# Pinning the auxiliary products in VectorE's queue behind the low part of a later weight load, in one decoder layer

## The chip, the cores and the metric

The kernel runs on one core of a Trainium2 chip. The metric is the device time of one execution in microseconds; a kernel is run several times and its median is what counts. TensorE is called PE in the profile, its weight loads PEld, VectorE DVE, ScalarE ACT, GpSimd POOL, and the engine that issues the DMAs SP (SPq is its queue).

## What is computed

One layer of a decoder trunk on 256 tokens of width 2048, in float32. Every weight is read once.

```
mod = silu(c) @ w_mod + b_mod              # 2048 -> 6*2048, one vector
sh1, sc1, g1, sh2, sc2, g2 = split(mod, 6)
h = rmsnorm(x) * (1 + sc1) + sh1
y = token_mixer(h)      # h @ w_in, sliding-window attention, gated linear attention, two branch products, @ w_out
x = x + g1 * rmsnorm(y)
h = rmsnorm(x) * (1 + sc2) + sh2
y = conv_ffn(h)         # h @ w_up (2*5632 columns), depthwise conv, silu * value, @ w_down
x = x + g2 * rmsnorm(y)
```

The first line is the auxiliary work: `mod` needs the 2048 x 12288 matrix `w_mod` only once, times one vector, and is done on VectorE, beside the matrix products on TensorE.

## The kernel before

**Weight parts.** All weights of the matrix products go through one stream of 528 parts of 128 x 1024 float32 (512 KB). `load` (line 245; DMAs at L251 and L253) brings a part into one of 4 `raw` buffers. `prep` (L255) splits it: ScalarE casts the high part (`hi`, L272, 3 buffers) and VectorE subtracts to get the low part (`lo`, L276, 3 buffers). TensorE then multiplies with both, as hi x hi, lo x hi and hi x lo: mostly 12 matmuls of 512 columns per part (`mm3`, L292 to L294), in the up projection 8 of 512 and 8 of 256 columns (`half_mm`, L343).

**Auxiliary halves.** Between the parts stream 224 halves of 128 x 1024 for the conditioning. 192 of them are halves of a row of `w_mod`: `mod_proc` (L207) multiplies one with the activated conditioning vector `cact` and sums along the row in one VectorE instruction, and after a row's second half L211 adds both sums and the bias into one column of `modc`. 32 are halves of a weight that a shift is multiplied with (`bias_proc`, L226). The first 64 halves go through 4 buffers named `early`; the later 160 go through the buffers `aux0` to `aux2`, three up to the up projection and two in it (the third is then used by the convolution). `aux_load` (L239) issues the DMA and `aux_proc` traces the product.

**The order.** A loop over q traces, in each turn, the matrix products of part q-3, the load of part q+3, `prep` of part q and, for the later halves, `aux_step(q)` after it: the products that are due by a table of positions, then as many auxiliary loads as there are free buffers. So on SP an auxiliary load of turn q stands right behind the load of part q+3.

The order on TensorE and SP is the order in which the program traces them (`manual_schedule`). On VectorE and ScalarE a scheduler sets it when the kernel is built, from its own estimate of when an instruction's inputs are there; what it gives is a fixed queue, and on the chip an instruction that waits holds up all behind it.

```
    for q in range(n + PR):
        if q >= PR:
            it["mm"](it, hf, *it.pop(("w", hf)))
        if q < n:
            while loaded < min(q + LD, n):
                load(*parts[loaded][:2])
            prep(*parts[q][:2])
            if not early:
                aux_step(q)
```

Of the kernel before, what the change touches and what calls it, by code (L numbers as in the profile page):

```python
# [9 lines left out]
F32 = mybir.dt.float32  # L10
# [3 lines left out]
ALU = mybir.AluOpType  # L14
# [24 lines left out]
def block_kernel(ctx: ExitStack, tc: tile.TileContext, x, cvec, pos, idn, cst, vec, vec2, gmask,  # L39
                 wgkup, wM, wS, wOG, wGK, wQK, wV, wGA, wGB, wBA, wBB, wO, wU, wD, out):  # L40
    nc = tc.nc
# [16 lines left out]
    def region(tag, shape, name, dt=F32):  # L58
        return big.tile(shape, dt, name=name, tag=tag)
# [7 lines left out]
    S = {}  # L67
# [162 lines left out]
    def aux_load(i):  # L230
        a = aux[i]
        if i < N_EARLY:
            if i == 0:
                S["early"] = region("E", [P, 4, HW], "early")
            raw = S["early"][:, i % 4]
        else:
            raw = auxb[i % (3 if i < N_PRE else 2)]
        a["raw"] = raw
        nc.sync.dma_start(out=raw, in_=a["src"][:, a["half"] * HW:(a["half"] + 1) * HW])  # L239

    def aux_proc(i):
        a = aux[i]
        (mod_proc if a["kind"] == "mod" else bias_proc)(a, a["half"], a.pop("raw"))

    def load(it, half):
        w = min(it["n"], HW)
        raw = rawp.tile([P, HW], F32, name="raw", tag="raw")
        it["raw", half] = raw[:, :w]
        if it.get("blk"):

            nc.sync.dma_start(out=raw.rearrange("p (f k) -> p f k", f=4), in_=it["src"][:, :, half * 256:half * 256 + 256])  # L251
        else:
            nc.sync.dma_start(out=raw[:, :w], in_=it["src"][:, half * HW:half * HW + w])  # L253

    def prep(it, half, defer=False):  # L255
        raw = it.pop(("raw", half))
        w = min(it["n"], HW)
        if it["hold"]:
            tag, new, o = it["hold"]
            if new and half == 0:  # L260
                S["held", tag] = region(tag, [P, 8 if tag == "H" else 4, HW], "held", F32R)
            hi, lo = S["held", tag][:, o + half], S["held", tag][:, o + 2 + half]
            split_to(hi, lo, raw)
        elif it["mm"] is gk_mm:

            hi, lo = hip.tile([P, HW], F32R, name="hi", tag="hi"), None
            hl = hi[:, :2 * w].rearrange("p (c s n) -> p c s n", s=2, n=16)
            split_to(hl[:, :, 0], hl[:, :, 1], raw.rearrange("p (c n) -> p c n", n=16))
        else:
            hi = hip.tile([P, HW], F32R, name="hi", tag="hi")  # L270
            lo = lop.tile([P, HW], F32R, name="lo", tag="lo")
            nc.scalar.copy(hi[:, :w], raw)  # L272
            if defer:
                it["w", half] = (hi, lo)
                return lambda: nc.vector.tensor_tensor(lo[:, :w], raw, hi[:, :w].bitcast(F32), op=ALU.subtract)
            nc.vector.tensor_tensor(lo[:, :w], raw, hi[:, :w].bitcast(F32), op=ALU.subtract)  # L276
        it["w", half] = (hi, lo)

    side = []
    at_bufs = []  # L280

    def side_step(n=1):
        for _ in range(n):
            while side:
                try:
                    next(side[0])
                    break
                except StopIteration:
                    side.pop(0)
# [6 lines left out]
    def split_to(hi_ap, lo_ap, src_ap):  # L296
        nc.scalar.copy(hi_ap, src_ap)  # L297
        nc.vector.tensor_tensor(lo_ap, src_ap, hi_ap.bitcast(F32), op=ALU.subtract)  # L298
# [104 lines left out]
    N_EARLY = len(aux)  # L403
# [469 lines left out]
    k = 0  # L873
# [266 lines left out]
    for grp in range(2):  # L1140
        for gi in range(NG):
            i = grp * NG + gi
# [12 lines left out]
    parts = []  # L1155
    for it in items:
        nh = -(-it["n"] // HW)
        parts += [(it, hf, hf == nh - 1) for hf in range(nh)]
    n = len(parts)
    assert n == n_parts[0]  # L1160
    loaded = aux_loaded = aux_done = 0
    late = []
    S["prep_up"] = lambda: prep(*late.pop(0)[:2], defer=True)

    def aux_step(q):

        nonlocal aux_loaded, aux_done
        while aux_done < len(aux) and aux[aux_done]["pos"] <= q:
            aux_proc(aux_done)
            aux_done += 1  # L1170
        while aux_loaded < min(len(aux), aux_done + (4 if aux_done < N_EARLY - 2 else 3 if aux_done < N_PRE - 2 else 2)):
            aux_load(aux_loaded)
            aux_loaded += 1

    for q in range(n + PR):
        if q >= PR:
            it, hf, last = parts[q - PR]
            if hf == 0 and "start" in it:
                it["start"]()
            it["mm"](it, hf, *it.pop(("w", hf)))  # L1180
            if it.get("wo") == 0 and hf == 0:
                side_step(2)
            if last:
                side_step(it["side"])
        if q < n:
            early = aux_done < N_EARLY
            while loaded < min(q + LD, n):
                if q == 0 and loaded % 2 == 0:
                    for _ in range(2):
                        aux_load(aux_loaded)  # L1190
                        aux_loaded += 1
                load(*parts[loaded][:2])
                loaded += 1
            if early:
                aux_step(q)
            if q >= PR and it.get("wo") == KC - 1:
                late += parts[q:q + 2] if hf == 0 else []
            else:
# [3 lines that stand above are left out]
# [83 lines left out]
```

## Time and profile before

| | us |
|---|---|
| median of 3 runs | 1598.68 (1593.10 to 1600.93) |
| the profiled execution | 1597.75, span 1595.6 |
| granted TensorE clock, mean of the span | 0.997 |

Busy time in the span:

| engine | us | share |
|---|---|---|
| PE (matmuls) | 1563.3 | 98% |
| PEld (weight loads, beside the matmuls) | 1293.2 | 81% |
| DVE | 1222.5 | 77% |
| ACT | 825.7 | 52% |
| POOL | 17.0 | 1% |

The DMA engines were busy for 72.9% of the span with the kernel's own transfers. A matmul's shown duration is longer than the distance to the next one, since they are pipelined: TensorE is full where matmuls start one after the other at an even distance, and an idle time in front of a matmul says what it waited for. In the views below, "[1.36 <-DVE lo L276]" behind an instruction says that its engine stood idle for 1.36 us before it and that the instruction at L276 ended that.

### The profile page before, as it was taken

How to read it: one execution, taken by the hardware profiler on the slowest of the kernel's cores; microseconds unless marked ns; L12 is line 12 of the kernel's file. 1: busy time of each engine (PE TensorE's matmuls, PEld its weight loads, DVE VectorE, ACT ScalarE, POOL GpSimd, SP SyncE). 2: the span in 40 equal slices, each digit the busy share in tenths (PEclk: the TensorE clock that was granted, in tenths of full speed). 3: DMA queues.
4: the chain of work that ended last, by engine and by line, in shares of the span. 5: the costliest groups of instructions: out<-in, count | busy, mean ns of one | idle time of the engine just before them, and what ended most of it. 6: DMA issues, size and time to landing. Idle time of an engine off the chain costs nothing.

```text
span 1595.6 us, 21287 instructions
## 1 busy us (share of the span) xinstructions
PE 1563.3 (98%) x7752; PEld 1293.2 (81%) x7752; DVE 1222.5 (77%) x1869; ACT 825.7 (52%) x1221; POOL 17.0 (1%) x35
## 2 busy tenths in 40 slices
PE   8999999999999999999999999999999999999997
PEld 6878888877767788777888888888778888888886
DVE  7999989968977778877778877777546777776446
ACT  5455565544477544443366555555335555555333
POOL 0000000000000000000000000000000000000001
PEclk9999999999999999999999999999999999999999
DMA  9999987877777799889935667677665555555554
GB/s 367 382 352 410 360 274 257 277 273 256 250 244 263 257 306 326 293 293 314 354 133 199 230 231 238 217 245 231 231 224 187 182 185 185 186 186 189 194 197 132
DMA packets 154841, 403.18 MB, mean 253 GB/s; under 512 B 12720, under 2 KB 70704, under 8 KB 154480
## 3 DMA queue, kind: packets, MB, share of 16 engines
q1 hardware_dynamic: 154736, 401.82, 72.9%
q8 instruction: 61, 1.00, 0.3%
q14 instruction: 44, 0.36, 0.1%
HBM read 399.68 MB, written 2.10 MB: 252 GB/s over the span
## 4 chain that ended last, share of the span: by engine, by line
PE 31%; DMA 22%; DVE 13%; issue 5%; ACT 2%; SPq 1%; POOL 0%; DVEq 0%; POOLq 0%; ACTq 0%
DMA aux<-in_wM_dram 21%; PE ps L343 16%; DVE lo L276 6%; PE ps L293 5%; PE ps L294 5%; PE ps L292 5%; DVE aux L207 2%; DMA raw<-in_wO_dram 1%; ACT hi L272 1%; SPq L251 0%; DVE aux L348 0%; DVE t2k L742 0%; DVE t2k L1093 0%; DVE y L1134 0%; SPq L253 0%
## 5 line engine op out<-in xcount | busy, mean ns | idle before, releaser
L272 ACT CAST hi<-raw 128x1024 fp32r<-128x1024 f32 x520 | 544.9, 1050 | 476.1 <-PE ps L294 366.9
L276 DVE TENSOR_TENSOR lo<-raw,hi 128x1024 fp32r<-128x1024 f32 x518 | 629.2, 1221 | 142.0 <-ACT hi L272 139.6
L343 PE MATMUL ps<-h,hi 128*128 128x512 f32 x1664 | 582.0, 398 | 1.0 <-DVE h L1051 1.0
L343 PE MATMUL ps<-h,lo 128*128 128x256 f32 x1664 | 451.0, 281 | 1.0 <-DVE lo L276 0.9
L343 PEld LDWEIGHTS ps<-h,hi 128*128 128x128 f32 x1664 | 306.4, 188 | 69.2 <-issue 1.3
L343 PEld LDWEIGHTS ps<-h,lo 128*128 128x128 f32 x1664 | 314.0, 189 | 13.8 <-DVE lo L276 4.4
L207 DVE SCALAR_TENSOR_TENSOR aux<-aux,cact 128x1024 f32<-128x1024 f32 x128 | 156.4, 1223 | 145.7 <-DMA aux<-in_wM_dram 145.6
L292 PE MATMUL ps<-hi,h 128*128 128x512 f32 x608 | 240.0, 395 | 1.6 <-ACT h L297 1.1
L293 PE MATMUL ps<-lo,h 128*128 128x512 f32 x608 | 237.4, 391 | 2.6 <-DVE lo L276 2.5
L294 PE MATMUL ps<-hi,h 128*128 128x512 f32 x608 | 237.1, 390 | 1.5 <-DVE h L298 0.8
L293 PEld LDWEIGHTS ps<-lo,h 128*128 128x128 f32 x608 | 114.2, 188 | 29.2 <-DVE lo L276 4.9
L294 PEld LDWEIGHTS ps<-hi,h 128*128 128x128 f32 x608 | 114.1, 188 | 26.9 <-DVE h L298 1.2
L292 PEld LDWEIGHTS ps<-hi,h 128*128 128x128 f32 x608 | 114.2, 188 | 26.7 <-ACT h L297 1.5
L293 PE MATMUL ps<-lo,act_ab 128*128 128x512 f32 x256 | 100.3, 392 | 2.2 <-DVE lo L276 2.2
L294 PE MATMUL ps<-hi,act_ab 128*128 128x512 f32 x256 | 99.7, 389 | 0.0
L292 PE MATMUL ps<-hi,act_ab 128*128 128x512 f32 x256 | 99.7, 389 | 0.0
L207 DVE SCALAR_TENSOR_TENSOR early<-early,cact 128x1024 f32<-128x1024 f32 x64 | 78.0, 1218 | 1.3 <-ACT cact L143 1.3
L347 ACT ACTIVATE aux<-ps 128x256 f32<-128x256 f32 x88 | 33.5, 380 | 75.4 <-PE ps L343 75.2
L1090 ACT ACTIVATE t2k<-aux,vc 128x256 f32<-128x256 f32 x88 | 52.8, 601 | 26.6 <-DVE aux L348 26.4
L348 DVE SCALAR_TENSOR_TENSOR aux<-ps,aux 128x256 f32<-128x256 f32 x88 | 37.0, 421 | 35.6 <-ACT aux L347 35.6
L293 PEld LDWEIGHTS ps<-lo,act_ab 128*128 128x128 f32 x256 | 48.0, 188 | 14.4 <-DVE lo L276 4.6
L292 PEld LDWEIGHTS ps<-hi,act_ab 128*128 128x128 f32 x256 | 48.0, 188 | 10.1
(270 smaller groups left out, 1614.2 us busy)
## 6 DMA issues: line engine op xcount, KB each, us to landing
raw<-in_wU_dram SPq DMA_DIRECT2D x176, 512.0 KB, 3.8
aux<-in_wM_dram SPq DMA_DIRECT2D x128, 512.0 KB, 6.0
raw<-in_wD_dram SPq DMA_DIRECT2D x88, 512.0 KB, 3.9
early<-in_wM_dram SPq DMA_DIRECT2D x64, 512.0 KB, 6.7
raw<-in_wS_dram SPq DMA_DIRECT2D x32, 512.0 KB, 6.4
raw<-in_wOG_dram SPq DMA_DIRECT2D x32, 512.0 KB, 7.0
aux<-in_wS_dram SPq DMA_DIRECT2D x32, 512.0 KB, 5.7
raw<-in_wQK_dram SPq DMA_DIRECT2D x32, 512.0 KB, 5.4
```

The lines of the kernel that those rows point to most:

```text
L207: nc.vector.scalar_tensor_tensor(out=raw, in0=raw, scalar=1.0, in1=cact[:, half * HW:(half + 1) * HW], op0=ALU.mult, op1=ALU.mult, accum_o ...
L272: nc.scalar.copy(hi[:, :w], raw)
L276: nc.vector.tensor_tensor(lo[:, :w], raw, hi[:, :w].bitcast(F32), op=ALU.subtract)
L292: nc.tensor.matmul(out=o, lhsT=lh, rhs=rh, start=start, stop=False)
L293: nc.tensor.matmul(out=o, lhsT=lh, rhs=rl, start=False, stop=False)
L294: nc.tensor.matmul(out=o, lhsT=ll, rhs=rh, start=False, stop=stop)
L343: nc.tensor.matmul(out=o, lhsT=w, rhs=m, start=c == 0 and o is ps, stop=c == nk - 1 and o is ps)
L347: nc.scalar.activation(o, ps[:, TOK:], AF.Copy, scale=scale)
L348: nc.vector.scalar_tensor_tensor(out=o, in0=ps[:, :TOK], scalar=scale, in1=o, op0=ALU.mult, op1=ALU.add)
L1090: nc.scalar.activation(z, u, AF.Identity, scale=w2, bias=vc2[:, W_CB + f:W_CB + f + 1])
```

## The change

For each part that is split by L276 the change remembers the instruction (`los`, by the part's number). When an auxiliary half is loaded it notes the turn `lq`; the product of a later half (`i >= N_EARLY`) is traced inside `tc.issue_after(...)`, which lets the scheduler put it on VectorE only behind the low part of part `lq + 3` or, where that one is not traced yet or has no such instruction, the last one before it. Part `lq + 3` is the one whose load stands right ahead of the half's own load on SP. No instruction is added or taken away; SP's, TensorE's and GpSimd's orders stay.

```diff
-        a["raw"] = raw
+        a["raw"], a["lq"] = raw, S.get("q", 0)
         nc.sync.dma_start(out=raw, in_=a["src"][:, a["half"] * HW:(a["half"] + 1) * HW])
 
     def aux_proc(i):
         a = aux[i]
-        (mod_proc if a["kind"] == "mod" else bias_proc)(a, a["half"], a.pop("raw"))
+        go = mod_proc if a["kind"] == "mod" else bias_proc
+        if i < N_EARLY:
+            return go(a, a["half"], a.pop("raw"))
+
+        with tc.issue_after(los[max(k for k in los if k <= a["lq"] + LAG)]):
+            go(a, a["half"], a.pop("raw"))
...
-            nc.vector.tensor_tensor(lo[:, :w], raw, hi[:, :w].bitcast(F32), op=ALU.subtract)
+            los[it["q"] + half] = nc.vector.tensor_tensor(lo[:, :w], raw, hi[:, :w].bitcast(F32), op=ALU.subtract).ins
...
+    LAG, los = 3, {}
...
+        it["q"] = len(parts)
...
+        S["q"] = q
```

Counted over the whole of VectorE's queue, 124 of the 160 later products stand behind more low parts than before: 89 behind two more, 14 behind one, 15 behind three and 6 behind four. The other 36 stand where they stood (27 of the bias, L226, and 9 of L207). The numbers of buffers and tiles behind the names are the same in both orders; L276 is L281 in the changed kernel, L298 is L304, L756 and L757 are L762 and L763, L909 is L915.

**Place A**, VectorE in the products of gate branch A (about 679 to 686 us). Before:

```order
L909 TENSOR_TENSOR dgr_5878<-ident_87,sp_5768 128x512
L211 SCALAR_TENSOR_TENSOR modc_107<-macc_5839,vc_96 128x1
L207 SCALAR_TENSOR_TENSOR aux1_103,macc_5907<-aux1_103,cact_113 128x1024
L207 SCALAR_TENSOR_TENSOR aux2_104,macc_5907<-aux2_104,cact_113 128x1024
L276 TENSOR_TENSOR lo_5857<-raw_5777,hi_5856 128x1024
L211 SCALAR_TENSOR_TENSOR modc_107<-macc_5907,vc_96 128x1
L276 TENSOR_TENSOR lo_5883<-raw_5795,hi_5882 128x1024
L276 TENSOR_TENSOR lo_5904<-raw_5833,hi_5903 128x1024
```

Now:

```order
L915 TENSOR_TENSOR dgr_5878<-ident_87,sp_5768 128x512
L207 SCALAR_TENSOR_TENSOR aux0_102,macc_5839<-aux0_102,cact_113 128x1024
L211 SCALAR_TENSOR_TENSOR modc_107<-macc_5839,vc_96 128x1
L281 TENSOR_TENSOR lo_5857<-raw_5777,hi_5856 128x1024
L281 TENSOR_TENSOR lo_5883<-raw_5795,hi_5882 128x1024
L207 SCALAR_TENSOR_TENSOR aux1_103,macc_5907<-aux1_103,cact_113 128x1024
L281 TENSOR_TENSOR lo_5904<-raw_5833,hi_5903 128x1024
L207 SCALAR_TENSOR_TENSOR aux2_104,macc_5907<-aux2_104,cact_113 128x1024
```

The two products of macc_5907 stood together ahead of lo_5857; now the first stands behind lo_5883 and the second behind lo_5904.

**Place B**, VectorE in the ordinary stretch of gate branch B (about 553 to 563 us). Before:

```order
L276 TENSOR_TENSOR lo_4883<-raw_4816,hi_4882 128x1024
L207 SCALAR_TENSOR_TENSOR aux2_104,macc_4925<-aux2_104,cact_113 128x1024
L211 SCALAR_TENSOR_TENSOR modc_107<-macc_4925,vc_96 128x1
L276 TENSOR_TENSOR lo_4904<-raw_4837,hi_4903 128x1024
L207 SCALAR_TENSOR_TENSOR aux0_102,macc_4985<-aux0_102,cact_113 128x1024
L276 TENSOR_TENSOR lo_4922<-raw_4857,hi_4921 128x1024
L276 TENSOR_TENSOR lo_4943<-raw_4880,hi_4942 128x1024
```

Now:

```order
L281 TENSOR_TENSOR lo_4883<-raw_4816,hi_4882 128x1024
L207 SCALAR_TENSOR_TENSOR aux1_103,macc_4925<-aux1_103,cact_113 128x1024
L281 TENSOR_TENSOR lo_4904<-raw_4837,hi_4903 128x1024
L281 TENSOR_TENSOR lo_4922<-raw_4857,hi_4921 128x1024
L207 SCALAR_TENSOR_TENSOR aux2_104,macc_4925<-aux2_104,cact_113 128x1024
L211 SCALAR_TENSOR_TENSOR modc_107<-macc_4925,vc_96 128x1
L281 TENSOR_TENSOR lo_4943<-raw_4880,hi_4942 128x1024
L207 SCALAR_TENSOR_TENSOR aux0_102,macc_4985<-aux0_102,cact_113 128x1024
```

The second product of macc_4925 stood behind lo_4883 and now stands behind lo_4922; the first of macc_4985 stood behind lo_4904 and now stands behind lo_4943: two low parts later each.

**Place C**, VectorE in the attention (about 461 to 472 us), where `dn` and `es` are the sums of the softmax and L757 their reciprocal. Before:

```order
L276 TENSOR_TENSOR lo_4097<-raw_3998,hi_4096 128x1024
L207 SCALAR_TENSOR_TENSOR aux2_104,macc_4131<-aux2_104,cact_113 128x1024
L211 SCALAR_TENSOR_TENSOR modc_107<-macc_4131,vc_96 128x1
L207 SCALAR_TENSOR_TENSOR aux0_102,macc_4234<-aux0_102,cact_113 128x1024
L756 TENSOR_TENSOR dn_4062<-dn_4062,es_4061 128x4
L757 RECIPROCAL dn_4062<-dn_4062 128x4
L207 SCALAR_TENSOR_TENSOR aux1_103,macc_4234<-aux1_103,cact_113 128x1024
```

Now:

```order
L281 TENSOR_TENSOR lo_4097<-raw_3998,hi_4096 128x1024
L207 SCALAR_TENSOR_TENSOR aux0_102,macc_4025<-aux0_102,cact_113 128x1024
L207 SCALAR_TENSOR_TENSOR aux1_103,macc_4131<-aux1_103,cact_113 128x1024
L211 SCALAR_TENSOR_TENSOR modc_107<-macc_4025,vc_96 128x1
L762 TENSOR_TENSOR dn_4062<-dn_4062,es_4061 128x4
L763 RECIPROCAL dn_4062<-dn_4062 128x4
L281 TENSOR_TENSOR lo_4128<-raw_4019,hi_4127 128x1024
```

Two products stand ahead of the softmax's sums as before, but each is the product of a half that was loaded two halves earlier than the one that stood there.

## Rows read from the trace of the kernel before

**Rows 1.** Timeline of TensorE, 553 to 580 us: start, duration, instruction.
```profile
562.42 0.39 PE L293 MATMUL ps<-lo,h 128*128 128x512 f32 x1
562.65 0.39 PE L294 MATMUL ps<-hi,h 128*128 128x512 f32 x1
```
**Rows 2.** Timeline of ScalarE in the same stretch.
```profile
555.59 1.05 ACT L272 CAST hi<-raw 128x1024 fp32r<-128x1024 f32 x1 [1.66 <-PE ps L294]
558.31 1.05 ACT L272 CAST hi<-raw 128x1024 fp32r<-128x1024 f32 x1 [1.67 <-PE ps L294]
```
**Rows 3.** Timeline of VectorE in the same stretch.
```profile
557.09 1.23 DVE L207 SCALAR_TENSOR_TENSOR aux<-aux,cact 128x1024 f32<-128x1024 f32 x1 [1.91 <-DMA aux<-in_wM_dram]
558.50 1.22 DVE L276 TENSOR_TENSOR lo<-raw,hi 128x1024 fp32r<-128x1024 f32 x1
```
**Rows 4.** Who waited for whom, 330 to 1200 us: total us, times, longest.
```profile
DVE aux L207 <- DMA aux<-in_wM_dram: 145.6, 87, 4.5
...
PEld ps L293 <- DVE lo L276: 15.6, 23, 1.8
...
PE ps L293 <- DVE lo L276: 7.4, 12, 1.4
...
PEld ps L343 <- DVE lo L276: 3.8, 8, 0.8
```
**Rows 5.** Timeline of TensorE and VectorE at place A.
```profile
683.51 0.39 PE L292 MATMUL ps<-hi,h 128*128 128x512 f32 x1
685.26 0.50 PE L293 MATMUL ps<-lo,h 128*128 128x512 f32 x1 [1.36 <-DVE lo L276]
...
682.84 1.23 DVE L207 SCALAR_TENSOR_TENSOR aux<-aux,cact 128x1024 f32<-128x1024 f32 x1 [1.38 <-DMA aux<-in_wM_dram]
...
683.99 1.22 DVE L276 TENSOR_TENSOR lo<-raw,hi 128x1024 fp32r<-128x1024 f32 x1
```
**Rows 6.** Timeline of SP, 553 to 563 us.
```profile
559.74 0.37 SPq L251 DMA_DIRECT2D raw<-in_wBB_dram  x1
560.15 0.51 SPq L239 DMA_DIRECT2D aux<-in_wM_dram  x1
```
**Rows 7.** DMA issues, whole span: each 512 KB, median us from issue to landing.
```profile
aux<-in_wM_dram SPq DMA_DIRECT2D x128, 512.0 KB, 6.0
...
raw<-in_wGB_dram SPq DMA_DIRECT2D x32, 512.0 KB, 4.8
```
**Rows 8.** Timeline of VectorE and TensorE, attention, about 417 us.
```profile
413.68 1.22 DVE L207 SCALAR_TENSOR_TENSOR aux<-aux,cact 128x1024 f32<-128x1024 f32 x1
...
416.44 1.21 DVE L276 TENSOR_TENSOR lo<-raw,hi 128x1024 fp32r<-128x1024 f32 x1
...
417.71 0.50 PE L293 MATMUL ps<-lo,ob 128*128 128x512 f32 x1 [0.90 <-DVE lo L276]
```
**Rows 9.** Timeline of VectorE, ScalarE and TensorE at place C.
```profile
467.04 1.22 DVE L207 SCALAR_TENSOR_TENSOR aux<-aux,cact 128x1024 f32<-128x1024 f32 x1 [3.30 <-DMA aux<-in_wM_dram]
...
468.38 0.18 DVE L757 RECIPROCAL dn<-dn 128x4 f32<-128x4 f32 x1
...
466.56 0.60 ACT L834 ACTIVATE tb<-ps 128x512 f32<-128x512 f32 x1
468.66 1.70 ACT L760 ACTIVATE t2k<-t2k,dn 128x256 f32<-128x256 f32 x4 [1.50 <-DVE dn L757]
...
470.88 1.71 PE L783 MATMUL ps<-t2k,qkv 128*64 128x512 f32 x2 [2.38 <-ACT t2k L772]
```
**Rows 10.** Windows: us, PE busy, PEld, DVE, ACT, POOL, PEclk, DMA, GB/s.
```profile
468.00:471.00 3.00, 0.62 (x3) 0.12 (x2) 1.61 (x5) 2.34 (x6) 0.00 (x0) 1.00 0.31 128
471.00:474.00 3.00, 3.00 (x8) 1.23 (x10) 2.56 (x5) 2.54 (x4) 0.00 (x0) 0.53 0.00 0
```
**Rows 11.** Windows, the same columns: gate branch A, and a stretch without auxiliary halves.
```profile
600.00:700.00 100.00, 97.50 (x434) 79.29 (x433) 80.96 (x116) 43.16 (x50) 0.00 (x0) 1.00 0.89 300
1480.00:1550.00 70.00, 70.00 (x311) 57.95 (x310) 31.84 (x26) 27.09 (x26) 0.00 (x0) 1.00 0.59 195
```

## The prediction

> **What bounds the kernel now.** I read the busy times first, then TensorE's and ScalarE's timelines in an ordinary stretch, then the list of who waited for whom, and then the places where TensorE itself stood still.
>
> TensorE sets the pace. In the products of gate branch B its matmuls of 512 columns start every 0.227 us (562.42, 562.65 and on) [rows 1]; a part has twelve, so it takes 12 x 0.227 = 2.72 us. ScalarE's casts keep exactly that step (555.59, 558.31), and each waits for TensorE, because it needs one of three `hi` buffers back [rows 2]. VectorE in the same stretch stands still for 1.91 us, until 557.09, for the landing of an auxiliary half, with the next low part queued behind it (place B) [rows 3], and nothing of this reaches TensorE. So of the 145.6 us that VectorE waits for such landings, 87 times, up to 4.5 us at once, nearly all costs nothing [rows 4].
>
> Why, and when not: a cast can begin when TensorE has finished the part three before, so two parts, 2 x 2.72 = 5.4 us, are left for the cast (1.05 us, [rows 2]) and the low part (1.22 us, [rows 3]). VectorE may be late by 5.4 - 1.05 - 1.22 = 3.2 us. Longer waits, two in a row, or a wait beside other work break through. Place A shows one: of two products in a row the second starts, after 1.38 us of waiting, at 682.84; the low part behind them starts only at 683.99, and TensorE, which needs it, stands from 683.51 to 685.26, that is 1.75 - 0.23 = 1.52 us too long [rows 5].
>
> How much of that is there? From 330 to 1200 us matmuls waited for a low part for 7.4 us, 12 times, in the three-product form of L293 [rows 4]. Weight loads, which should run ahead of the matmuls, waited 15.6 us there and 3.8 us in the up projection [rows 4]. The true loss lies between: at place A the shown idle time is 1.36 us and the loss 1.52, 0.16 more [rows 5]. For twelve stalls that is 7.4 + 12 x 0.16 = 9.3 us. The remaining weight-load waits, 23 + 8 - 12 = 19, are mostly too short to show on a matmul; I take 0.1 us each, 2 us. So about 11 us of TensorE's time, between 7.4 and 19.4 us, are lost to late low parts.
>
> **The change, part by part.** Nothing is added or removed; 124 products move, most behind two more low parts.
>
> *The waits.* Before, the load of a half stands 0.4 us behind that of part q+3 on SP [rows 6], which goes out when the low part of q-1 has freed its raw buffer. The half lands 6.0 us after issue (median) [rows 7], but its product stood behind the low part of q+1 (place B), two parts or 5.4 us later: 0.4 + 6.0 - 5.4 = 1.0 us late, near the mean wait of 145.6 / 87 = 1.7 us. The change gives it two parts more, 5.4 us, above the longest wait of 4.5 us. I expect nine tenths of the 145.6 us to go.
>
> *What is late next.* The auxiliary buffers come free two parts later, so SP now waits for a product before a load. With three buffers, four or five low parts lie between two products in one buffer. That is at least 4 x 2.72 = 10.9 us, against product 1.22, issue 0.5 and landing 6.0 us, together 7.7 us: 3.2 us to spare [rows 3, 6, 7]. Behind that load SP has only the load of part q+4, which needs the low part of q in any case. I cost it at nothing; if the landing grows by more than 3.2 us the old wait is back, at most its present price.
>
> *A rule against this.* The pin takes part q+3 as a sign that the half, issued next, will be there as well. The rows: the raw parts of gate branch B land after 4.8 us, halves after 6.0, issued 0.4 later, so 1.6 us behind the part [rows 6, 7]; cast and low part take 2.3 us [rows 2, 3], but only when nothing holds them up. In the Trainium skill, "DMA: Bandwidth & Descriptors" (Queues, rings and completion order) says that completion is not first in, first out for one issuing engine. By that rule alone the pin would give no cover at all and the sum would be 0 instead of the 11.5 us below. The rows give cover of another sort, the two parts of TensorE's time ahead of the product, so I keep the sum and make the missing cover a rival.
>
> *The stalls.* Without the wait the low parts are done within 2.3 us of their cast's start, 3 us ahead of need. Of the 11 us I take back 10. The one at 417.71 stays, as an example of another father: VectorE is there in the rope work, the only product nearby started at 413.68 without a wait, and still the low part of 416.44 was late [rows 8]. Bounds: 0, if all stalls were of that kind, and 19.4 us, all weight-load waits.
>
> *The attention (place C).* Before, the second of two products waited 3.30 us for its landing (467.04), and the softmax's reciprocal behind it was ready at 468.56; ScalarE waited 1.50 us for it, and TensorE 2.38 us at 470.88 [rows 9]. Then TensorE's granted clock was 0.53 from 471 to 474 us, that is 1.2 GHz for most of it instead of 2.4, after it had been busy for 0.62 of the 3 us before [rows 10]. Now two products stand there whose halves were loaded two halves earlier, about 2.4 us of work. The sums are then ready before ScalarE has finished the sigmoid that started at 466.56 and takes 0.60 us, so ScalarE goes on at 467.2 instead of 468.66: 1.5 us sooner. I take 1.5 us; bounds 0 and 1.5 + 3 x (1 - 0.53) = 2.9 us, if the clock stays up as well.
>
> *Sum.* 10 + 1.5 = 11.5 us of gain; bounds 0 and 19.4 + 2.9 = 22.3. The profiled execution took 1597.75 us, 0.9 below the median of 1598.68; 1597.75 - 11.5 = 1586.3, and 1587.2 beside the median. I forecast **1587 us**, 0.7% faster.
>
> **The rivals.** A measurement of this kernel tells 0.5%, 8 us, from no change; that lies between 1590.7 and 1606.7.
>
> *Most stalls have another father* (0.33). The waits go, but low parts are still late where VectorE has its own backlog: it was 81% busy in gate branch A [rows 11]. For it: 417.71 [rows 8]; against it: at place A the wait stands right before the late part [rows 5]. A third comes back: 4 us, 1594.
>
> *The pin gives no cover* (0.04). Halves go out later and land as late as before relative to their product; the 145.6 us stay: 1598. Against it, the 3.2 us to spare.
>
> *A hole in the attention* (0.07), slower. At place C two products stand between a low part and the softmax's sums. If landings there end later than ScalarE's exponentials, every one of the six softmax units has a hole like that at 470.88: 2.4 us of standing and 1.4 us of slow clock [rows 9, 10]. Five more than now are 19 us, less 6 us of stalls that still vanish: 1612. It decides from four such holes on. Against it: these products' halves were issued two halves earlier than those that waited.
>
> *TensorE has more room than its timeline shows* (0.02). Its weight loads fill 81% of the span (79.3% of branch A). In the Trainium skill, "Perfetto Trace Analysis" (Identifying the Most-Contended Engine) says to judge TensorE's headroom by this share and by the useful work, not by matmul busy time. Were the rest room, all of VectorE's waits would come back: 1598.7 - 145.6 = 1453. The rows speak against it: where no auxiliary half is under way weight loads fill 57.95 of 70 us, 83% [rows 11], so 83 is the ceiling for this shape, and the 0.227 us step is the same with and without waits.
>
> **How the numbers follow.** My forecast has 0.54, the rivals 0.33, 0.04, 0.07 and 0.02. Faster by over 0.5%: 0.54 + 0.02 = 0.56. Within 0.5%: 0.33 + 0.04 = 0.37. Slower: 0.07. The range runs from 1578 (most of the upper bounds) to 1600 (no gain, and half the scatter of the runs before on top); the forecast's own range is 1578 to 1590.7.
>
> **What would show it.** Right: VectorE's wait for auxiliary landings below 20 us; matmuls' wait for low parts at L293 below 2 us; SP waiting for L207; the casts still every 2.72 us; the hole near 470 us 1.5 us shorter or gone. Wrong: that VectorE wait gone but the matmuls' wait still over 5 us (another father), the VectorE wait still over 100 us (no cover), or new idle time of TensorE before L769 and L783 with a low granted clock (holes).

## The result and the profile after

The changed kernel takes 1578.11 us (median; 1577.9 to 1579.53) against 1599.81 us for the kernel before in the same session: ratio 0.9873, 95% interval 0.9842 to 0.9904. Repeated later, on another chip, it gave 0.9844 (0.9815 to 0.9872). The profiled spans are 1575.8 and 1595.6 us, 19.8 us apart. The forecast was 1587 us, with 11.5 us of gain: the direction holds and the time lies in the range, 0.1 us above its low end of 1578, but the gain is nearly twice the sum. The scatter shrank as well: on that other chip 11 runs of the kernel before took 1595.93 to 1612.29 us and 6 of the changed one 1578.4 to 1580.59 us.

The busy times on the page, before and then after:

```profile
PE 1563.3 (98%) x7752; PEld 1293.2 (81%) x7752; DVE 1222.5 (77%) x1869; ACT 825.7 (52%) x1221; POOL 17.0 (1%) x35
```
```profile
PE 1554.4 (99%) x7752; PEld 1295.0 (82%) x7752; DVE 1230.9 (78%) x1869; ACT 828.5 (53%) x1221; POOL 17.3 (1%) x35
```

TensorE stood for 1595.6 - 1563.3 = 32.3 us before and stands for 1575.8 - 1554.4 = 21.4 us now: 10.9 us less. The other 8.9 us of the 19.8 went out of its *busy* time, with the same 7752 matmuls. That is the first thing to see here, because the forecast was mostly made from idle time.

The costliest groups of VectorE and of the low matmul after the change (busy, mean ns of one | idle before, releaser):

```profile
L281 DVE TENSOR_TENSOR lo<-raw,hi 128x1024 fp32r<-128x1024 f32 x518 | 632.9, 1223 | 239.0 <-ACT hi L277 236.7
...
L299 PE MATMUL ps<-lo,h 128*128 128x512 f32 x608 | 236.7, 389 | 0.0
L207 DVE SCALAR_TENSOR_TENSOR aux<-aux,cact 128x1024 f32<-128x1024 f32 x128 | 155.7, 1218 | 0.0
```

Who waited for whom from 330 to 1200 us, after, in answer to [rows 4]:

```profile
DVE lo L281 <- ACT hi L277: 148.6, 173, 4.5
...
PEld ps L299 <- DVE lo L281: 0.8, 2, 0.6
...
PE ps L299 <- DVE lo L281: 0.2, 1, 0.2
```

VectorE's 145.6 us of waiting for landings are gone to the last microsecond. It now waits for casts instead, and a cast waits for TensorE, as it should when TensorE sets the pace. The weight loads' 15.6 us and the matmuls' 7.4 us of waiting for low parts are 0.8 and 0.2 us. The chain that ended last, by engine, after:

```profile
PE 69%; DVE 3%; ACT 1%; issue 1%; POOL 0%; DVEq 0%; POOLq 0%; ACTq 0%
```

Before, 21.2% of that chain was the landing of auxiliary halves and TensorE's matmuls were less than a third of it.

VectorE after, in the stretch that was place A:

```profile
669.33 1.23 DVE L281 TENSOR_TENSOR lo<-raw,hi 128x1024 fp32r<-128x1024 f32 x1 [0.19 <-ACT hi L277]
672.05 1.22 DVE L281 TENSOR_TENSOR lo<-raw,hi 128x1024 fp32r<-128x1024 f32 x1 [1.49 <-ACT hi L277]
673.19 1.22 DVE L207 SCALAR_TENSOR_TENSOR aux<-aux,cact 128x1024 f32<-128x1024 f32 x1
```

The low part comes first and the product, whose half has long landed, follows without idle time. ScalarE's casts keep their step (548.58, 551.29, 554.01: every 2.72 us).

**Where the 20 us came from.** Both kernels run the same 7752 matmuls in the same order, so the start of the k-th in one trace can be set against the k-th in the other. From one row of this table to the next the after trace gained:

| stretch of the trace before, us | gain, us |
|---|---|
| 330 to 460 (rope, first attention units) | 3.5 |
| 460 to 480 (the hole, place C) | 3.1 |
| 480 to 760 (attention, gate branches) | 7.2 |
| 760 to 860 | 0.7 |
| 860 to 1060 (up projection) | 1.4 |
| 1060 to 1200 | 4.2 |
| before 330 | -0.3 |
| after 1200 | 0.0 |

From 330 to 1200 us the sum is 20.1 us: 3.1 at the hole and 17.0 elsewhere, at 36 places. Of these, 16 gave at least 0.5 us each (13.4 together), 11 gave 0.2 to 0.5 (3.5), and 9 less (0.8); one place lost 0.4, and small drifts make up the rest. About 14.0 of the 17.0 us came at matmuls that take a low part. Another 2.6 came at five that take something else (L623 twice, L769, L863, and L292 at 739.60 us, which waited for `mg`).

**The hole.** TensorE at place C after, and the two windows in answer to [rows 9, 10] (us, PE busy, PEld, DVE, ACT, POOL, PEclk, DMA, GB/s):

```profile
466.15 1.07 PE L789 MATMUL ps<-t2k,qkv 128*64 128x512 f32 x2 [0.86 <-ACT t2k L778]
```
```profile
465.00:470.00 5.00, 4.14 (x20) 2.31 (x20) 2.93 (x4) 4.91 (x8) 0.00 (x0) 1.00 0.24 88
470.00:475.00 5.00, 5.00 (x26) 4.14 (x25) 5.00 (x15) 3.10 (x6) 0.00 (x0) 1.00 0.53 172
```

The wait fell from 2.38 to 0.86 us, 1.52 less, and TensorE's granted clock no longer fell behind it: 1.00 where it had been 0.53 [rows 10]. TensorE had stood 2.4 us before the fall then; 0.86 us of standing was followed by none now.

### The profile page after: what moved, and what is told of

Its sections match the earlier page's. It is cut to its first block, busy times and chain, and to the rows that moved or that the text cites. A ratio compares the mean times of both kernels' runs of the same rounds, so it can differ in the third digit from the quotient of the medians.

```text
span 1575.8 us, 21297 instructions
## 1 busy us (share of the span) xinstructions
PE 1554.4 (99%) x7752; PEld 1295.0 (82%) x7752; DVE 1230.9 (78%) x1869; ACT 828.5 (53%) x1221; POOL 17.3 (1%) x35
## 4 chain that ended last, share of the span: by engine, by line
PE 69%; DVE 3%; ACT 1%; issue 1%; POOL 0%; DVEq 0%; POOLq 0%; ACTq 0%
PE ps L349 31%; PE ps L298 12%; PE ps L299 12%; PE ps L300 12%; DVE lo L281 0%; PE ps L742 0%; PE ps L789 0%; DVE y L1140 0%; ACT aux L1008 0%; PE ps L775 0%; PE ps L1033 0%; DVE aux L207 0%; DVE h L1057 0%; PE ps L921 0%; DVE y L1131 0%
## 5 line engine op out<-in xcount | busy, mean ns | idle before, releaser
L281 DVE TENSOR_TENSOR lo<-raw,hi 128x1024 fp32r<-128x1024 f32 x518 | 632.9, 1223 | 239.0 <-ACT hi L277 236.7
L298 PE MATMUL ps<-hi,h 128*128 128x512 f32 x608 | 240.0, 395 | 1.6 <-ACT h L303 1.0
L299 PE MATMUL ps<-lo,h 128*128 128x512 f32 x608 | 236.7, 389 | 0.0
L207 DVE SCALAR_TENSOR_TENSOR aux<-aux,cact 128x1024 f32<-128x1024 f32 x128 | 155.7, 1218 | 0.0
L298 PEld LDWEIGHTS ps<-hi,h 128*128 128x128 f32 x608 | 114.1, 188 | 26.7 <-issue 1.5
L299 PEld LDWEIGHTS ps<-lo,h 128*128 128x128 f32 x608 | 114.2, 188 | 24.4 <-issue 0.7
L298 PE MATMUL ps<-hi,act_ab 128*128 128x512 f32 x256 | 99.6, 389 | 0.0
L299 PE MATMUL ps<-lo,act_ab 128*128 128x512 f32 x256 | 99.6, 389 | 0.0
L207 DVE SCALAR_TENSOR_TENSOR early<-early,cact 128x1024 f32<-128x1024 f32 x64 | 78.0, 1218 | 1.2 <-ACT cact L143 1.2
L299 PEld LDWEIGHTS ps<-lo,act_ab 128*128 128x128 f32 x256 | 48.1, 188 | 10.1
L300 PEld LDWEIGHTS ps<-hi,act_ab 128*128 128x128 f32 x256 | 48.0, 188 | 9.9
L298 PEld LDWEIGHTS ps<-hi,act_ab 128*128 128x128 f32 x256 | 48.0, 188 | 9.9
```

The source lines that it names most:

```text
L207: nc.vector.scalar_tensor_tensor(out=raw, in0=raw, scalar=1.0, in1=cact[:, half * HW:(half + 1) * HW], op0=ALU.mult, op1=ALU.mult, accum_o ...
L281: los[it["q"] + half] = nc.vector.tensor_tensor(lo[:, :w], raw, hi[:, :w].bitcast(F32), op=ALU.subtract).ins
L298: nc.tensor.matmul(out=o, lhsT=lh, rhs=rh, start=start, stop=False)
L299: nc.tensor.matmul(out=o, lhsT=lh, rhs=rl, start=False, stop=False)
L300: nc.tensor.matmul(out=o, lhsT=ll, rhs=rh, start=False, stop=stop)
```

## The experiments

Ratios are against the kernel before, timed on the same chip each time, since its median went from 1599.81 to 1605.31 us between sessions. Where two variants are compared with each other, they were run on one chip, unless it is said otherwise.

**One part of cover only.**

```diff
-    LAG, los = 3, {}
+    LAG, los = 1, {}
```

> The change with LAG = 1: a product may stand behind the low part of part lq+1, where the scheduler put most of them by itself; 142 of the 160 later products stand where they stood before. Cover theory (the gain is the landing time that the two more parts cover): VectorE still waits 120 to 150 us for auxiliary landings, the time is that of the kernel before within 0.4%, 1594 to 1603 us. Rival (the gain comes from the dependency as such, from the scheduler's changed order on ScalarE and VectorE beside the products): at least a third of the gain is there, below 1592 us.

Measured: 1595.52 us, ratio 0.9945 (0.9924 to 0.9965). From 330 to 1200 us:

```profile
DVE aux L207 <- DMA aux<-in_wM_dram: 98.1, 77, 3.2
...
PEld ps L349 <- DVE lo L281: 6.7, 8, 1.6
PEld ps L299 <- DVE lo L281: 6.5, 12, 1.6
```

The time is within what was expected, the landing wait below it. With LAG 1, 142 of the 160 later products stand where they stood before. The pin with so little distance brings 0.55% instead of 1.3 to 1.6; two thirds of the landing wait stay, and with them the waits for low parts. Even the 0.55% is hardly the pin as such: 13 of the 18 products that do move stand between 330 and 480 us, and by the starts of its matmuls this kernel gains 6.9 us there, as the change does (6.6). From 480 to 760 us, where the other five stand, it gains 2.0 us against 7.2. So the distance between load and product does the work.

**Two parts of cover.**

```diff
-    LAG, los = 3, {}
+    LAG, los = 2, {}
```

> The change with LAG = 2: most products stand behind one more low part (2.72 us of TensorE's pace) than before instead of two. Cover theory: of the 87 waits of before 14 were longer than 2.72 us, by 10.9 us in sum, so VectorE waits about 10 us, up to 25; such short waits lie within the 3.2 us that VectorE may be late, TensorE's waits for low parts stay below 2 us, and the time is 1577 to 1582 us, as with LAG = 3. Rival (the gain grows with how far products are moved away from the low parts they stood in front of): half of the gain, 1586 to 1592 us.

Measured: 1575.62 us, ratio 0.9823 (0.9797 to 0.9848); VectorE waited for a landing once, 1.6 us. Time and wait both lie below what was expected. Two parts, 5.4 us of TensorE's time, are enough for loads that land in 6 us. In the same session LAG 1 took 20 us more, which makes the step from one part to two the one that decides. Whether two parts beat three is taken up below.

**Only the late products pinned** (halves from 190 on, the up projection), and **only the earlier ones** (64 to 189):

```diff
-        if i < N_EARLY:
+        if i < N_PRE - 2:
```

> Only the products from half 190 on are pinned (the up and the first down projection, 2 buffers); all earlier ones stand as in the kernel before. Start for start TensorE gained 5.6 us behind 850 us with the whole change. Cover theory: that part comes alone, 1593 to 1596 us against 1599.8, and the waits behind 850 us are gone while those between 330 and 800 us stay at 75 to 85 us. Rival (the stalls of one stage come from lateness carried over from the stage before): less than 2 us, above 1597 us.

```diff
-        if i < N_EARLY:
+        if i < N_EARLY or i >= N_PRE - 2:
```

> Only the products of halves 64 to 189 are pinned (up to the up projection). Cover theory: TensorE gains 14 us up to 850 us as with the whole change and nothing behind it; about 1584 to 1587 us. Rival (stages hang together): the parts of this run and of the one with only the late products pinned do not add up to the whole within 3 us.

Measured: the late ones alone 1596.23 us (0.2 above the range expected), ratio 0.9961 (0.9937 to 0.9985); by the starts of its matmuls the gain behind 850 us is 5.6 us, as much as the whole change gains there (1.4 + 4.2). The earlier ones alone gave 1588.8 us in one run (1584 to 1587 expected); up to 850 us its matmuls gain 13.9 us (whole change: 14.5 by 860 us), but behind that it loses 5. The waits of the second kernel, 330 to 1200 us:

```profile
DVE aux L207 <- DMA aux<-in_wM_dram: 70.0, 29, 5.0
PEld ps L349 <- DVE lo L281: 7.6, 7, 1.7
...
PE ps L349 <- DVE lo L281: 4.7, 6, 1.3
```

The gain is spread over both parts and they add up. In the second kernel the unpinned products of the up projection wait up to 5.0 us, and matmuls of its form stand for 4.7 us, against 0.7 in the trace before. That leaving off in the middle costs more than never beginning does not follow, since the unpinned order scatters there by itself. From 860 to 1200 us VectorE and ScalarE have the order of before in four traces: the kernel before, LAG 1, this kernel, and the next experiment. Start for start they lose 5.6, 4.6, 10.4 and 10.6 us there to the changed kernel. The nine other traces whose products are pinned there lose 0.0 us.

**Only the products around the hole pinned** (halves 114 to 123).

```diff
-        if i < N_EARLY:
+        if not 114 <= i < 124:
```

> Only the ten products of halves 114 to 123 are pinned, those around the attention's hole at 470 us. Cover theory: the wait of 3.3 us ahead of the softmax's sums goes, TensorE's standing there falls from 2.4 to about 0.9 us, its clock stays at the upper level, and TensorE gains 3 to 3.5 us between 460 and 480 us and little elsewhere: 1595.5 to 1597.5 us. Rival (the hole is ScalarE's, by its sigmoids and exponentials): TensorE still stands for over 2 us there and the clock falls, 1599 to 1600 us.

Measured: 1600.59 us, ratio 0.9979 (0.9956 to 1.0003): as a time it can't be told from no change, and it lies outside the 1595.5 to 1597.5 us expected. In the trace the hole is gone: by the starts of its matmuls this kernel gains 3.5 us between 450 and 500 us, and the granted clock stays up.

```profile
465.00:470.00 5.00, 5.00 (x24) 4.13 (x23) 2.13 (x7) 4.96 (x13) 0.00 (x0) 1.00 0.77 229
470.00:475.00 5.00, 4.16 (x19) 1.69 (x18) 1.56 (x2) 5.00 (x10) 0.00 (x0) 1.00 0.41 157
```

Against the trace before, the hole is worth about 3 us, at the upper of the bounds given (2.9). The rest of this run's trace shows the stalls that the kernel before has too, some of them larger, so its time shows little of the 3 us. But the old order does not always pay them. With only the late products pinned, VectorE and ScalarE stand at place C as in the kernel before, and VectorE waits 2.94 us there:

```profile
467.89 1.23 DVE L207 SCALAR_TENSOR_TENSOR aux<-aux,cact 128x1024 f32<-128x1024 f32 x1 [2.94 <-DMA aux<-in_wM_dram]
```
```profile
471.74 1.07 PE L789 MATMUL ps<-t2k,qkv 128*64 128x512 f32 x2 [1.14 <-ACT t2k L778]
```

TensorE stood for 1.14 us instead of 2.38, the clock stayed up, and this trace gains 3.1 us between 450 and 500 us without a pin there. ScalarE waited 0.17 us for the reciprocal instead of 1.50, since its sigmoid ended 2.2 us later than in the trace before and VectorE's wait only 0.9 us later. In one trace the old order lost 3.1 us at the hole to the changed kernel, in the other 0.3.

**Two auxiliary buffers from half 128 on, instead of three.**

```diff
-            raw = auxb[i % (3 if i < N_PRE else 2)]
+            raw = auxb[i % (3 if i < 128 else 2)]
...
-        while aux_loaded < min(len(aux), aux_done + (4 if aux_done < N_EARLY - 2 else 3 if aux_done < N_PRE - 2 else 2)):
+        while aux_loaded < min(len(aux), aux_done + (4 if aux_done < N_EARLY - 2 else 3 if aux_done < 126 else 2)):
```

> The change with two auxiliary buffers instead of three from half 128 on up to the up projection. Three low parts lie then between two products in one buffer, 8.2 us, against 7.7 us for product, issue and landing: 0.5 us to spare instead of 3.2. Cover theory: landings over 6.5 us come late, VectorE waits 15 to 60 us again between 500 and 800 us, most of it within the 3.2 us that it may be late, so the time is 1579 to 1586 us. Rival (the third buffer does not matter, the order alone does): below 5 us of waits, 1576 to 1579 us.

Measured: 1586.94 us, ratio 0.9874 (0.9841 to 0.9906). VectorE's landing wait did not come back (1.2 us, 3 times, where 15 to 60 us were expected), and the time is above the 1579 to 1586 us expected. LAG 3 was not run on this chip, and the ratio is that of the change's first session (0.9873), so the price is read from the times alone (1578 and 1579 us for LAG 3 on two other occasions) and from the traces. It appears elsewhere: SP's queue, then the casts, 330 to 1200 us:

```profile
SPq L239 <- DVE aux L207: 143.7, 57, 7.6
SPq L239 <- DVE modc L211: 62.0, 24, 7.8
```
```profile
ACT hi L277 <- DMA raw<-in_wO_dram: 18.7, 7, 8.0
ACT hi L277 <- DMA raw<-in_wGA_dram: 11.7, 5, 2.7
```

With the change itself SP waits 38.0 and 22.5 us in the first two rows, casts wait 10.6 us for `in_wO` (3.9 at most), and none waits for `in_wGA`. An auxiliary load that waits for its buffer stands ahead of the next part's load on SP, so the *part* lands late. Not every such wait costs time: between 600 and 700 us, among the parts of `in_wGA`, this kernel gains 3.9 us as the change does. Of the 9.0 us by which its profiled span is longer than that of the change, 4.9 are lost at one place. The load of a part of `in_wO` goes out at 741.56 us, behind an auxiliary load that had waited for its buffer and two loads of `x`; its cast starts 12.3 us later (10.8 with the change), and TensorE stands for it:

```profile
740.19 0.33 SPq L239 DMA_DIRECT2D aux<-in_wM_dram  x1
740.57 0.90 SPq L936 DMA_DIRECT2D xr<-in_x_dram  x2
741.56 0.69 SPq L258 DMA_DIRECT2D raw<-in_wO_dram  x1
```
```profile
753.89 1.04 ACT L277 CAST hi<-raw 128x1024 fp32r<-128x1024 f32 x1 [8.02 <-DMA raw<-in_wO_dram]
754.99 0.51 PE L298 MATMUL ps<-hi,mg 128*128 128x512 f32 x1 [2.05 <-ACT hi L277]
```

The clock fell to 1.2 GHz for 3.4 us there, which is about 1.7 of the 4.9 us (an estimate: half of the time).

**Far more lag.**

```diff
-    LAG, los = 3, {}
+    LAG, los = 6, {}
```

> The change with LAG = 6: products stand as late as the trace allows, mostly three to five low parts later than before. Cover theory: nothing is left to cover, and the next limit (buffers that come free later, so loads that go out later) is not reached, since four or five low parts still lie between two products in one buffer: 1576 to 1581 us, VectorE's wait for landings below 5 us. Rival (every part that a product is pushed back delays the next load and so the stream): slower than LAG = 3 by 3 us or more.

Measured: 1585.54 us, ratio 0.9872 (0.9844 to 0.99); no landing wait at all, but above the 1576 to 1581 us expected and slower than three parts seemed to be. To compare lags without the chips between them, LAG 3, 2 and 6 ran on one chip:

> The change itself again, to stand on the same chip as the three others of this job. Against the kernel before on this chip 0.987 to 0.988; VectorE waits 0 us for landings. No theory is tested by it alone.

> Products behind the low part of lq + 2. My theory: two parts of TensorE's time (5.4 us) are needed as cover for a load that lands in 6 us, and LAG 2 gives them; one part less of delay lets the products leave VectorE earlier where it is filled (attention), so 2 to 3 us faster than LAG 3 on the same chip (0.998), and VectorE waits under 3 us for landings. Rival: the difference seen between jobs was the chip's; then LAG 2 and LAG 3 agree within 0.1%. Rival: each part of lag is cover that pays; then LAG 2 is 1 to 3 us slower than LAG 3.

> Products behind the low part of lq + 6. My theory: the landing wait is already 0 at LAG 3, so more lag brings nothing, and buffers that come free three parts later hold SP back, so the loads bunch and a few low parts are late: 1 to 6 us slower than LAG 3 on the same chip, matmuls' and weight loads' wait for low parts at L299 3 to 6 us. Rival (more cover is better): 0 to 3 us faster than LAG 3. Rival (the chip explains what the earlier job showed): the same within 0.1%.

| LAG | us, median (all runs) | ratio to before | VectorE's landing wait, us | SP waits for L207 and L211, us |
|---|---|---|---|---|
| 2 | 1576.70 (1575.27 to 1577.71) | 0.9827 (0.9799 to 0.9855) | 2.1 | 13.0 + 3.1 |
| 3 | 1579.45 (1578.4 to 1580.59) | 0.9844 (0.9815 to 0.9872) | 0 | 38.0 + 22.5 |
| 6 | 1586.54 (1586.08 to 1590.06) | 0.9894 (0.9865 to 0.9922) | 0 | 200.9 + 81.8 |

The ratio of LAG 3 lies a little below the 0.987 to 0.988 expected. No runs of one row reach into another. Lag costs once the landing is covered: 2.75 us (0.17%) from 2 to 3, 7.1 us (0.45%) from 3 to 6, the last a little beyond the 1 to 6 us expected. The mechanism at LAG 6 is that of the two buffers: SP and then ScalarE, 330 to 1200 us,

```profile
SPq L239 <- DVE aux L207: 200.9, 68, 8.3
SPq L239 <- DVE modc L211: 81.8, 28, 7.5
```
```profile
ACT hi L277 <- DMA raw<-in_wO_dram: 23.7, 11, 7.4
ACT hi L277 <- DMA raw<-in_wBB_dram: 8.1, 4, 2.7
```

and one of the stalls it makes, a part that lands late, its cast, and the matmul that stands for the low part:

```profile
422.27 1.04 ACT L277 CAST hi<-raw 128x1024 fp32r<-128x1024 f32 x1 [2.06 <-DMA raw<-in_wBB_dram]
423.49 0.50 PE L299 MATMUL ps<-lo,ob 128*128 128x512 f32 x1 [1.43 <-DVE lo L281]
```

LAG 6 loses 1.3 us to LAG 3 there, and 4.9 between 700 and 850 us: 2.8 of them at the place just shown for the two buffers (756 us here), 1.2 at 729 us before L869, and the rest in smaller pieces. Between LAG 2 and LAG 3 the largest difference is what was left of the hole: LAG 2 has no wait of L789 for `t2k` at all (LAG 3: 0.9 us) and gains 1.9 us between 450 and 500 us; 1.6 us more come from 100 to 150 us, where the clock fell to 1.2 GHz for 3.4 us in the LAG 3 run and not in the LAG 2 run. In that early stretch no pinned product stands, so this part is not the lag's. A fall of that length lowers a run's mean granted clock by 0.001. Among the runs with 0.997 the medians of LAG 3 and LAG 2 are 1579.5 and 1577.4 us, among those with 0.998 they are 1578.4 and 1575.9 us, so 2.1 to 2.5 us are left for the lag.

**More work on VectorE.** A copy in place (0.68 us) ahead of each of the 160 later products; the second kernel only from half 124 on, 100 copies, behind about 470 us.

```diff
+            nc.vector.tensor_copy(a["raw"], a["raw"])
             go(a, a["half"], a.pop("raw"))
```

> The change with one more VectorE instruction of 128 x 1024 in front of each of the 160 later products, a copy in place, 0.6 to 1.2 us each, 100 to 190 us of work in all. Cover theory (what cost time were waits longer than 3.2 us, not VectorE's load): mostly hidden, at most 5 us slower than the change, 1577 to 1583 us. Rival (TensorE's stalls came from VectorE's backlog, of which the waits were only a part): 10 us or more slower, above 1588 us, with TensorE's waits for low parts back over 8 us.

```diff
+            i >= 124 and nc.vector.tensor_copy(a["raw"], a["raw"])
             go(a, a["half"], a.pop("raw"))
```

> The copy in place ahead of each product only from half 124 on (100 copies of 0.68 us, 68 us of VectorE time, all behind about 470 us). My theory: there VectorE has room, what cost time before was waiting ahead of low parts at 250 to 450 us, where VectorE is over 90% busy; so within 4 us of LAG 3 on the same chip. Rival (TensorE pays for any VectorE work that stands in this queue, at the rate of the earlier run, 10 to 12 us for 109 us): 6 to 8 us slower than LAG 3.

Measured: all copies 1598.38 us, ratio 0.996 (0.9938 to 0.9982), about 12 us slower than LAG 6 and the two buffers on the same chip, a miss: I had taken VectorE to have more room than that. The time is the rival's, but not its sign: matmuls and weight loads waited 2.9 and 4.5 us for low parts from 330 to 1200 us, 7.4 together and not over 8, and most of the loss lies before 330 us. The late copies 1581.35 us (1579.6 to 1582.15), 1.9 us or 0.12% above LAG 3 on the same chip, with overlapping runs. So 68 us of VectorE work behind 470 us cost about 2 us, and the 41 us ahead of it the rest. By the starts of its matmuls the first kernel falls behind the kernel before by 8 us between 250 and 300 us, by 3 more up to 350 and by 3 between 400 and 450 us, and from 450 us on gains as the change does, but for 2.9 us less between 700 and 850. Up to 330 us it is the small chain of the V stage that is late; its waits, 225 to 460 us:

```profile
PE ps L589 <- DVE bf L565: 6.9, 4, 2.5
...
PE ps L300 <- DVE lo L282: 2.5, 1, 2.5
```

The kernel after has neither wait there. Three of these stalls, of 2.45, 2.01 and 2.52 us (at 277, 327 and 436 us), each went with a fall of the clock to 1.2 GHz, for 6.8, 3.4 and 3.4 us. If half of that time is lost, about 6.8 of the 14 us are the slow clock (an estimate). The first of them, and the clock (last but two) around it:

```profile
276.92 0.69 PE L589 MATMUL ps<-bf 128*64 128x64 f32 x4 [2.45 <-DVE bf L565]
```
```profile
275.00:285.00 10.00, 8.08 (x35) 6.98 (x36) 7.24 (x14) 1.67 (x4) 0.00 (x0) 0.66 0.65 237
```

VectorE was already busy for 47.86 of the 50 us from 250 to 300 in the kernel after, so copies there have nowhere to go: from 200 to 300 us it is busy for 92.7 us, and the 17 copies of 0.69 us put there would make that 104 of 100 us (an estimate). Below that, full is not the same as late: the change itself loses nothing at 96% from 250 to 300 us, and with the late copies VectorE is busy for 144 of 150 us, again 96%, and TensorE stands for 1.0 us:

```profile
250.00:300.00 50.00, 50.00 (x306) 43.51 (x305) 47.86 (x89) 25.91 (x44) 0.00 (x0) 1.00 0.79 275
```
```profile
600.00:750.00 150.00, 149.00 (x674) 123.38 (x673) 144.39 (x209) 65.07 (x73) 0.00 (x0) 1.00 0.94 317
```

(The first line is of the change, the second of the kernel with the late copies.) So the 8 us came where VectorE was asked for more than it has, and a short chain ran through it to TensorE (`bf`, L589); which of the two is needed the runs do not separate. The late copies speak for the chain: what they lose to the change, 0.9 us at 727 us and 0.8 at 811, is lost at two short chains (L299 waiting for `mg`, and L1034, whose `diag` comes from VectorE), nothing at a low part.

## Why the prediction was right, and its size wrong

*The waits go.* Nine tenths of 145.6 us were forecast; all went. The reason given holds: the distance behind the load counts, since one part of cover (LAG 1) keeps 98.1 us of wait and two parts (LAG 2) keep 2.1.

*SP costs nothing.* Right for three buffers and LAG 3: SP's wait before an auxiliary load rose to 60.5 us, and TensorE lost at most the 2 us or so by which LAG 2 is faster. The 3.2 us "to spare" are not confirmed: with two buffers the same working leaves 0.5 us, and the halves still landed in time (1.2 us of waits). What ended first is the order on SP. I had written that the load of part q+4, behind that of a half, "needs the low part of q in any case"; with two buffers, or three parts more of lag, it is held up until the half's buffer is free, and the part lands late. The step foresaw the wrong victim: I had written that the old wait would be back then; in the runs it is the casts that wait.

*The rule on completion order* ("DMA: Bandwidth & Descriptors" in the Trainium skill, section "Queues, rings and completion order": no first-in-first-out completion for one issuer). By it alone the pin would have been worth nothing. VectorE's wait of 0.0 us against 145.7 shows that the distance in time did the covering; nothing in the runs speaks about the order of completion itself.

*The stalls: 10 us forecast, about 14 measured, and 2.6 more that the sum had no term for.* This is the step that failed in size, and with the hole it explains why the gain was nearly twice the sum. The range held the time by 0.1 us, which is luck: its low end was set at "most of the upper bounds", not worked out. I built it as "twelve stalls that is 7.4 + 12 x 0.16" and "0.1 us each" for 19 other weight-load waits. Two things were missing for the low parts, and a third came from elsewhere.

First, a stall costs more than its idle time and its 0.16 us. One place of the kernel before, TensorE's timeline:

```profile
531.01 0.48 PE L292 MATMUL ps<-hi,ob 128*128 128x512 f32 x1
531.91 0.50 PE L293 MATMUL ps<-lo,ob 128*128 128x512 f32 x1 [0.42 <-DVE lo L276]
532.25 0.40 PE L294 MATMUL ps<-hi,ob 128*128 128x512 f32 x1
532.49 0.40 PE L292 MATMUL ps<-hi,ob 128*128 128x512 f32 x1
```

The idle time shown is 0.42 us. The matmul starts 0.90 us after its neighbour instead of 0.227, and the next one starts another 0.34 later instead of 0.227. That is 0.67 + 0.11 = 0.78 us, nearly twice the 0.42 that is seen. The 0.34 was there at place A as well (685.26, then 685.61), one row behind the row I quoted. This part of the loss is booked as busy time: at the 27 places of at least 0.2 us the starts gained 16.7 us where 9.7 us of idle time had been shown, so about 7 of the 8.9 us above hid in this way (27 x (0.16 + 0.11) would be 7.3), and the slow clock at the hole (3.1 - 1.5) is about 1.6.

Second, the small weight-load waits were not small. Of the 27 places 22 are matmuls that take a low part, more than the twelve that the row of the matmuls' own wait lists. The 14.0 us lie between my 11 and the weight loads' 15.6 + 3.8 = 19.4 us, so neither list prices the loss.

Third, 2.6 us came back at five places where TensorE waited for something else (L623, L769, L863, `mg`). The sum knew late low parts and place C alone.

*"The one at 417.71 stays, as an example of another father."* It did not stay: after the change that stall is gone (1.2 us; 0.4 of it is lost again at 423 us). In the order of the changed kernel the rope operations there stand otherwise, too: VectorE does one low part at 411.81 and the next at 414.09 with a single product between, where five rope operations and a product had stood between two of them (412.21 and 416.44). A pin moves what the scheduler puts around it. So the father was another one, the rope work, as I had read it, but that was no sign that the stall would stay, and the chance of 0.33 leaned on a weak row.

*The hole: 1.5 us forecast, 3.1 measured.* The wait shrank by 1.52 us as worked out, and the clock stayed at 2.4 GHz as well, which I had put only into the bound. Both are measured against one trace of the old order; the other one with the same order there lost only 0.3 us, so the size of this term is partly that of the execution.

*The rivals.* Another father: it put the time at 1594 us, 16 us above the result. No cover: the wait is gone. A hole in every softmax unit: TensorE's wait before L789 is down to 0.9 us, none stands before L775, and no fall of the clock stands between 330 and 1200 us. TensorE with more room (1453 us): the weight loads' share went from 81 to 82% while all of VectorE's wait went, and only 20 of the 145.6 us came back; with TensorE full from 600 to 700 us it is 83.02 of 100 us, so 83% is the ceiling here. The Trainium skill ("Perfetto Trace Analysis", section "Identifying the Most-Contended Engine") judges headroom by this share and by the useful work; read as room up to 100%, the share would have misled here. Of these four, the first three are excluded by the trace after alone; the size of the gain is settled by the matmul starts and by the two halves of the change, which add up.

*What stays open.* That LAG 2 is better than LAG 3 was expected from the first run and held in the second; of the 2.1 to 2.5 us that are left when the clock is equal, 1.9 have a place (the hole). Why the unpinned order loses 4.6 us behind 860 us in one execution and 10.6 in another is not shown. Nor is it shown why the clock falls in one execution and not in another.

## What to carry to other kernels

Work that waits for a transfer and stands ahead of the critical work on the same engine belongs behind as many units of that work as the landing takes, and no more: here two parts of 2.72 us for a landing of 6 us, since each further one holds the buffer, and with it the queue that loads the critical parts. Price a stall of a pipelined engine by the distance of its instructions' starts against the steady step, through the instruction after it as well, not by its idle time: here idle time showed 10.9 of 20 us. Whether an engine has room is read from what waits behind it, and from what is asked of it: 96% busy cost at most 1 us, 104 us asked of 100 (an estimate) cost 8 us, part of it by the slow clock, and what the late copies cost was lost at short chains and not at low parts. One trace of an order that waits for landings is one draw: the same order lost 4.6 to 10.6 us in one stretch.

## What had not been expected of the hardware

- After a stall the next 512-column matmul started 0.34 us later instead of 0.227, at all the places looked at (417.71, 531.91, 685.26, 1122.85), so each stall costs 0.11 us more.
- The granted clock fell to 1.2 GHz for 3.4 us once TensorE had stood for 2.38 us, and did not fall after 0.86 us of standing at the same place. But the standing alone does not decide it. At about 109 us TensorE stands for 1.02 to 1.07 us and shortly after for 0.81 us in all 14 traces, and none of the edits moves anything there. In seven of them (LAG 1, the repeat of LAG 3 and LAG 6 among them) the clock then fell for 3.4 us at about 111 us, which sets a run back by some 1.6 us. In the other seven it did not. LAG 3 in its repeat and LAG 2 on the same chip, TensorE and then the window behind it (the clock is the last number but two):

```profile
108.66 0.50 PE L298 MATMUL ps<-hi,h 128*128 128x512 f32 x1 [1.02 <-ACT h L303]
```
```profile
112.00:115.00 3.00, 3.00 (x10) 2.39 (x9) 3.00 (x7) 1.18 (x3) 0.00 (x0) 0.62 1.00 324
```
```profile
108.86 0.50 PE L298 MATMUL ps<-hi,h 128*128 128x512 f32 x1 [1.04 <-ACT h L303]
```
```profile
112.00:115.00 3.00, 3.00 (x15) 2.49 (x14) 3.00 (x5) 0.97 (x3) 0.00 (x0) 1.00 0.99 311
```
- The parts of gate branch B land in 5.6 us instead of 4.8 in the kernel after [rows 7], those of gate branch A in 5.5 instead of 4.7 and those of `in_wBB` in 5.1 instead of 3.9, the halves in 5.9 as before (6.0); no product waits for a half, and one cast 2.3 us for a part of that branch (one, 1.8 us, before).
